# A hybrid decoder layer on one core: one load for the final norm, norm steps spaced wider, output matrices in the buffers of u, and another order of the instructions

## The chip, the cores and the metric

The kernel runs on one core of one Trainium2 chip. Its time is the device time in microseconds of one execution; lower is better. TensorE (PE) multiplies, with its weight loads (PEld) beside it; VectorE (DVE), ScalarE (ACT) and GpSimd (POOL) work elementwise; SyncE (SP) issues most of the transfers (DMA). Each engine takes its instructions in the order of its own list, so an instruction that waits holds up all that stands behind it on that engine.

## The reference

One layer on 16 learned tokens and 2048 given ones, 1024 features, in fp32:

```python
hn = rms_norm(h, norm_mix_g)
b_gate, c_gate, v, u = split(hn @ w_in)             # 512 features each
conv_out = b_gate * causal_dwconv(c_gate * v)        # width 3
ssm_out = s5_group_ssm(u, ...)                       # 32 groups of 16, complex diagonal state of 64, GELU, half-GLU
mixed = concat(rms_norm(conv_out), rms_norm(ssm_out))
h = h + mixed @ w_out
up = causal_dwconv(rms_norm(h, norm_ffn_g) @ w_up) + bias    # 2 x 2816
h = h + (silu(up[:, :2816]) * up[:, 2816:]) @ w_down
y = rms_norm(h, norm_final_g)[:, 16:]
```

## The kernel before

Features lie on partitions, tokens along the free axis. Each fp32 product is three matmuls of rounded halves: with a value split into a high part h_ and the rest l_ (weights: wh_ and wl_), it is h by wh, h's rest by wh, and h by wl's rest (L138, L139, L142 in `product`; L1391 to L1393 in `form`). SP loads raw weights wr_, ACT rounds them to wh_ (L247), DVE subtracts to get wl_ (L109 is the helper `tt` of all DVE's two-operand sums and products). Raw weights have three buffers, split ones four.

The program has these stages. (1) u of block 0, the gated convolution of block 0 (cv, cc, cb, with cvt, vs, tc on DVE) and, beside it, the coefficients of the state space model: tables, transposes tp (L615) copied to tq and written to mat_d in DRAM, then eight slots of products w1, w2 and their difference vm, written to mat_d as well. (2) u and convolution of the other two blocks, with the scan in eight batches 0 to 7 beside it: `ssm_load_out` brings the output matrices mo of a batch, py (L806, L807) multiplies by them. (3) The output projection's convolution part pk, the GLU pg, and the projection po of three token blocks. (4) The gated MLP over three token blocks, each in 22 units of 128 features in groups of 4, 4, 4, 3, 3, 4. `up` of a unit is seven products (b11, t4, t1, t2, b22, b21, t3, a Strassen-like scheme) of 12 matmuls into the PSUM tiles xy and pz; z, g and v are the copies, the convolution and the gate on DVE and ACT, ah and al the split result. After the first unit of the next group, `down` multiplies the finished group (dn); ACT copies it to ev, and POOL adds ev to h_d in DRAM. So a stretch of three or four ups takes turns with one of down.

Norms are generators, run a step at a time between other work (`prep.step`): squares sq summed on DVE, a matmul st with ones, sv, a square root on ACT and POOL (sr), a diagonal dg, a matmul sb that spreads it, rs. A norm's name tells which: c4 is piece of block 2's input, ms and mc the two groups of the mix, f10 the MLP norm of block 1, first half, y00 the final norm of block 0, first half. `prep_rs` makes the sums of the MLP norm, `prep_mlp` scales the four quarters v_b11 to v_b22 of the next block and splits them and their sums (h_t, l_t, h_b, l_b), `finish` makes the final norm of blocks 0 and 1 (`finish_last` that of block 2).

The order of each engine's list does not come from the order of the code alone: a list scheduler places instructions by a model of the engines, with the order of the code as priority.

Of the kernel before, what the change touches and what calls it, by code (L numbers as in the profile page):

```python
# [17 lines left out]
P = 128  # L18
# [39 lines left out]
def layer_kernel(ctx, tc, xq, pk, w_in, w_glu, w_out, w_up, w_down, ssm_s, ssm_m, y):  # L58
# [49 lines left out]
    def tt(out, a, b, op):  # L108
        V.tensor_tensor(out, a, b, op=op)  # L109
# [83 lines left out]
    def inv_rms_at(ss, starts, nfeat, n, name, out=None, keep=False):  # L193
# [8 lines left out]
        for j, o in enumerate(starts):  # L202
            V.tensor_scalar(dg[:sl, o : o + sl], ident[:sl, :sl], r[:sl, j : j + 1], None, op0=ALU.mult)
        yield
        pb = aux_tile(f"sb_{name}")
        T.matmul(pb[:, :n], ones[:sl, :], dg[:sl, :n], start=True, stop=True)
# [7 lines left out]
    def inv_rms_from(srcs, n, name, out=None):  # L214
# [6 lines left out]
        yield  # L221
        if xg is not None:
            yield
            yield
        for t in ts:
# [65 lines left out]

    prep, ssm = Side(), Side()
    SQ = 2

# [429 lines left out]
    def ssm_load_out(b):  # L724
        g0 = b * GB
        mo = a1.tile([P, GB, 2, P], F32, tag="mo", name=f"mo_{b}")
        dma(out=mo, in_=mat_d[:, g0 : g0 + GB, 1:3, :])
        mos[b] = mo

# [68 lines left out]
    def ssm_out(b):  # L798
# [3 lines left out]
        for q in range(PB):  # L802
            ps = mm_tile(f"py_{b}_{q}")
            for par in range(2):
                g = 2 * q + par
                T.matmul(ps[:, par, :NC], mo[:, g, 1, :], ub[:, g, :], start=True, stop=False)  # L806
                T.matmul(ps[:, par, :NC], mo[:, g, 0, :], yy[b][:, q, par, :], start=False, stop=True)  # L807
            S.activation(gb[:, 2 * q : 2 * q + 2, :], ps[:, :, :NC], AF.Gelu_apprx_tanh)
# [267 lines left out]
    prep.add(prep_glu(0, hg[0]), prep_glu(1, hg[1], **xh2))  # L1076
    prep.lanes = 1
    kept = conv_part(0)
# [260 lines left out]
    def finish(b):  # L1339
        for c in range(2):  # L1340
            s0, n = y_at(b, c)
            srcs = [h_d[:, i * 4 : i * 4 + 4, s0 : s0 + n] for i in range(2)]
            rs = yield from inv_rms_from(srcs, n, f"y{b}{c}")
            yield
            for i in range(2):
                a = half_tile(n, f"y_{b}_{c}_{i}", tag="sq", bufs=4)
                dma(out=a, in_=srcs[i])
                yield
                yield
                for k in range(4):  # L1350
# [27 lines left out]
    for b in range(3):  # L1378
# [119 lines left out]
        for ci, (f0, nk) in enumerate(chunk_of):  # L1498
# [3 lines left out]
            for f in range(f0, f0 + nk):  # L1502
                up(f, f == f0 + nk - 1 and ci == last)
                if f == f0 and ci:
                    for ms in first_pair:
                        down(ci - 1, ms)
                        work()
                        prep.step(2 * len(ms))
            if ci == last:
# [122 lines left out]
```

## Time and profile before

| | us |
|---|---|
| median of three runs | 2228.49 (2227.72 to 2231.98) |
| profiled execution | 2233.74 |
| its span | 2232.0 |
| PE busy | 2128.2 |
| DVE busy | 1684.8 |
| ACT busy | 1101.2 |
| mean granted clock of PE | 0.979 |

Busy time of PE counts each matmul from its start to a modelled end, and neighbours overlap, so idle time and waits tell more than the busy share. The profiled execution is 5.2 us above the median, and sums are made against it. In the page's rows a group is a line, engine, operation and tile, with the idle time just ahead of it and what ended that.

### The profile page before, as it was taken

The page shows a single profiled execution, that of the slowest core. Times are in us where ns is not written, and L with a number is a line of the kernel's source. Part 1 is how long each engine was busy: PE and PEld are TensorE (multiplying, and loading weights), DVE is VectorE, ACT ScalarE, POOL GpSimd, SP SyncE. Part 2 cuts the span into 40 slices and gives each one's busy share as a digit, 9 for nine tenths or more (in the row PEclk, how much of TensorE's full clock was granted, in tenths as well). Part 3 has the DMA queues.
Part 4 walks back from the last instruction along what each step waited for, and adds up shares of the span by engine and source line. Part 5 has one row for each costly group of instructions (what it writes and reads, how often), then busy time and mean ns, then how long its engine had stood idle before and what let it go on. Part 6 is the DMA issues. An engine that isn't in the chain of part 4 may idle for free.

```text
span 2232.0 us, 33123 instructions
## 1 busy us (share of the span) xinstructions
PE 2128.2 (95%) x13012; PEld 2065.3 (93%) x13012; DVE 1684.8 (75%) x2507; ACT 1101.2 (49%) x1651; POOL 151.9 (7%) x174
## 2 busy tenths in 40 slices
PE   8997999989899999999999898999998999999997
PEld 7997999989898999999998898999998999999996
DVE  8796499848957798686768777787767879667776
ACT  4135333227523464554555555455555555555554
POOL 0000000000000001101110010100110010110000
PEclk9898999999999999999999999999999999999998
DMA  7376544352475435525554453734554463554463
GB/s 246 99 220 162 135 149 153 113 168 61 141 248 188 149 89 146 130 63 125 127 133 121 120 161 113 211 85 110 129 130 122 125 191 91 134 118 99 100 174 103
DMA packets 174909, 305.85 MB, mean 137 GB/s; under 512 B 32480, under 2 KB 108960, under 8 KB 174624
## 3 DMA queue, kind: packets, MB, share of 16 engines
q1 hardware_dynamic: 154016, 251.98, 36.5%
q0 software_dynamic: 19584, 47.52, 12.7%
q10 hardware_dynamic: 1152, 4.23, 0.5%
q8 instruction: 102, 1.67, 0.3%
q14 instruction: 55, 0.45, 0.1%
HBM read 219.86 MB, written 83.82 MB: 136 GB/s over the span
## 4 chain that ended last, share of the span: by engine, by line
PE 44%; issue 32%; DVE 11%; DMA 6%; POOL 3%; ACT 3%; SPq 0%; POOLq 0%; DVEq 0%; ACTq 0%
PE xy L1391 5%; PE xy L1393 4%; PE xy L1392 4%; PE dn L138 3%; PE dn L139 3%; PE dn L142 3%; POOL h_d L1492 3%; PE pz L1391 2%; PE pz L1393 2%; PE pz L1392 2%; PE po L138 1%; PE po L142 1%; PE po L139 1%; DMA wr_up<-in_w_up 1%; PE cc L138 1%
## 5 line engine op out<-in xcount | busy, mean ns | idle before, releaser
L109 DVE TENSOR_TENSOR wl_up<-wr_up,wh_up 128x1024 fp32r<-128x1024 f32 x198 | 241.5, 1221 | 156.0 <-ACT wh_up L247 154.0
L138 PE MATMUL dn<-ah,wh_dn 128*128 128x344 f32 (+1 forms) x1024 | 326.7, 323 | 10.4 <-ACT ah L247 8.9
L139 PE MATMUL dn<-al,wh_dn 128*128 128x344 f32 (+1 forms) x1024 | 326.0, 322 | 0.1
L247 ACT ACTIVATE wh_up<-wr_up 128x1024 fp32r<-128x1024 f32 x198 | 209.4, 1058 | 207.5 <-PE dn L139 53.9
L1391 PE MATMUL xy<-h_t,wh_up 128*128 128x344 f32 (+1 forms) x792 | 264.5, 334 | 13.3 <-ACT z L1429 7.5
L1393 PE MATMUL xy<-h_t,wl_up 128*128 128x344 f32 (+1 forms) x792 | 254.5, 321 | 0.0
L1392 PE MATMUL xy<-l_t,wh_up 128*128 128x344 f32 (+1 forms) x792 | 254.0, 321 | 0.0
L142 PE MATMUL dn<-ah,wl_dn 128*128 128x344 f32 (+1 forms) x1024 | 247.8, 321 | 0.0
L138 PEld LDWEIGHTS dn<-ah,wh_dn 128*128 128x128 f32 x1024 | 193.9, 190 | 14.8 <-ACT ah L247 9.7
L1492 POOL DMA_DIRECT2D h_d<-ev x136 | 118.3, 870 | 1271.4 <-ACT ev L1488 1266.4
L139 PEld LDWEIGHTS dn<-al,wh_dn 128*128 128x128 f32 x1024 | 194.3, 190 | 1.3 <-DVE al L109 0.8
L1391 PE MATMUL xy<-h_b,wh_up 128*128 128x344 f32 (+1 forms) x528 | 176.5, 336 | 10.6 <-ACT ev L1488 7.9
L1391 PEld LDWEIGHTS xy<-h_t,wh_up 128*128 128x128 f32 x792 | 150.2, 190 | 32.2 <-ACT z L1436 14.9
L142 PEld LDWEIGHTS dn<-ah,wl_dn 128*128 128x128 f32 x1024 | 178.5, 190 | 0.0
L1392 PE MATMUL xy<-l_b,wh_up 128*128 128x344 f32 (+1 forms) x528 | 169.5, 321 | 0.0
L1393 PE MATMUL xy<-h_b,wl_up 128*128 128x344 f32 (+1 forms) x528 | 168.3, 321 | 0.0
L1392 PEld LDWEIGHTS xy<-l_t,wh_up 128*128 128x128 f32 x792 | 150.8, 190 | 0.0
L1393 PEld LDWEIGHTS xy<-h_t,wl_up 128*128 128x128 f32 x792 | 150.7, 190 | 0.0
L247 ACT ACTIVATE wh_dn<-wr_dn 128x512 fp32r<-128x512 f32 (+1 forms) x144 | 85.5, 594 | 124.8 <-issue 43.1
L115 DVE SCALAR_TENSOR_TENSOR g<-z,pv,g 128x688 f32<-128x688 f32 (+1 forms) x132 | 122.0, 925 | 19.6 <-ACT g L1396 18.9
L109 DVE TENSOR_TENSOR wl_dn<-wr_dn,wh_dn 128x512 fp32r<-128x512 f32 (+1 forms) x144 | 92.3, 643 | 48.9 <-ACT wh_dn L247 47.8
L115 DVE SCALAR_TENSOR_TENSOR v<-z,pneg,v 128x688 f32<-128x688 f32 (+1 forms) x132 | 122.2, 926 | 9.3 <-ACT v L1396 8.1
(401 smaller groups left out, 5359.8 us busy)
## 6 DMA issues: line engine op xcount, KB each, us to landing
wr_up<-in_w_up SPq DMA_DIRECT2D x132, 512.0 KB, 5.4
h_d<-ev POOLq DMA_DIRECT2D x88, 344.0 KB, 7.1
wr_dn<-in_w_down SPq DMA_DIRECT2D x96, 256.0 KB, 2.6
wr_cw<-in_w_in SPq DMA_DIRECT2D x36, 512.0 KB, 4.4
h_d<-ev POOLq DMA_DIRECT2D x48, 336.0 KB, 6.6
x_c<-in_xq SPq DMA_DIRECT2D x16, 688.0 KB, 6.0
wr_dn<-in_w_down SPq DMA_DIRECT2D x48, 192.0 KB, 2.4
xr<-in_xq SPq DMA_DIRECT2D x24, 344.0 KB, 4.2
```

What stands on the lines that cost most here:

```text
L109: V.tensor_tensor(out, a, b, op=op)
L115: V.scalar_tensor_tensor(out=out, in0=a, scalar=s, in1=b, op0=ALU.mult, op1=ALU.add)
L138: T.matmul(ps[c], hi[:, k, :], xh, start=k == 0, stop=False)
L139: T.matmul(ps[c], hi[:, k, :], xl, start=False, stop=False)
L142: T.matmul(ps[c], lo[:, k, :], xh, start=False, stop=k == nk - 1)
L247: S.activation(hi, t, AF.Copy)
L1391: T.matmul(ps, hi[:, j, :], xh[:, j, :], start=start and j == 0, stop=False, **kw)
L1392: T.matmul(ps, hi[:, j, :], xl[:, j, :], start=False, stop=False, **kw)
L1393: T.matmul(ps, lo[:, j, :], xh[:, j, :], start=False, stop=j == 3, **kw)
L1492: G.dma_start(out=h_d[:, m, s0 : s0 + no], in_=ev, accum_op=ALU.add)
```

## The change

Five edits in the code, and one in how it is ordered. From `conv_part` on a norm yields once more between dg and sb (`slack`). After its load of h a norm that reads from DRAM always yields four times before it squares. The output matrices mo of odd batches come in two halves into two buffers of u (`ut`), those of even ones into the buffer of mo as before. The final norm of blocks 0 and 1 loads each half of h once, squares it into other tiles (ysq) and scales what it has loaded; before, h was loaded once for the squares and once more to be scaled. Beside down one step of the side work is made for each tile and not two. The last line lets the scheduler place the instructions by a timeline simulation, which changes the order on every engine.

```diff
--- before.py
+++ after.py
@@ -202,6 +202,8 @@
         for j, o in enumerate(starts):
             V.tensor_scalar(dg[:sl, o : o + sl], ident[:sl, :sl], r[:sl, j : j + 1], None, op0=ALU.mult)
         yield
+        if slack:
+            yield
         pb = aux_tile(f"sb_{name}")
         T.matmul(pb[:, :n], ones[:sl, :], dg[:sl, :n], start=True, stop=True)
         if keep:
@@ -219,9 +221,8 @@
             dma(out=ts[i], in_=src)
         yield
         yield
-        if xg is not None:
-            yield
-            yield
+        yield
+        yield
         for t in ts:
             S.activation(t, t, AF.Square)
         a, b = ts
@@ -290,6 +291,7 @@
                 self.step()
 
     prep, ssm = Side(), Side()
+    slack = False
     SQ = 2
 
     class Stream:
@@ -723,9 +725,17 @@
 
     def ssm_load_out(b):
         g0 = b * GB
-        mo = a1.tile([P, GB, 2, P], F32, tag="mo", name=f"mo_{b}")
-        dma(out=mo, in_=mat_d[:, g0 : g0 + GB, 1:3, :])
-        mos[b] = mo
+        if b % 2 == 0:
+            mo = a1.tile([P, GB, 2, P], F32, tag="mo", name=f"mo_{b}")
+            dma(out=mo, in_=mat_d[:, g0 : g0 + GB, 1:3, :])
+            mos[b] = [mo[:, g] for g in range(GB)]
+            return
+        mos[b] = []
+        for i in range(0, GB, 2):
+            t = cvp.tile([P, NJ, 86], F32, tag="ut", bufs=2, name=f"mo_{b}_{i}").rearrange("p j x -> p (j x)")
+            mo = t[:, : 4 * P].rearrange("p (g m c) -> p g m c", g=2, m=2)
+            dma(out=mo, in_=mat_d[:, g0 + i : g0 + i + 2, 1:3, :])
+            mos[b] += [mo[:, 0], mo[:, 1]]
 
     def ssm_in(b):
 
@@ -803,8 +813,8 @@
             ps = mm_tile(f"py_{b}_{q}")
             for par in range(2):
                 g = 2 * q + par
-                T.matmul(ps[:, par, :NC], mo[:, g, 1, :], ub[:, g, :], start=True, stop=False)
-                T.matmul(ps[:, par, :NC], mo[:, g, 0, :], yy[b][:, q, par, :], start=False, stop=True)
+                T.matmul(ps[:, par, :NC], mo[g][:, 1, :], ub[:, g, :], start=True, stop=False)
+                T.matmul(ps[:, par, :NC], mo[g][:, 0, :], yy[b][:, q, par, :], start=False, stop=True)
             S.activation(gb[:, 2 * q : 2 * q + 2, :], ps[:, :, :NC], AF.Gelu_apprx_tanh)
         S.dma_start(out=by_group(g_d)[:, g0 : g0 + GB, :], in_=gb)
 
@@ -1074,7 +1084,7 @@
     hos = [[] for _ in range(3)]
     load_glu()
     prep.add(prep_glu(0, hg[0]), prep_glu(1, hg[1], **xh2))
-    prep.lanes = 1
+    prep.lanes, slack = 1, True
     kept = conv_part(0)
     prep.lanes = 2
     until(hg[0])
@@ -1339,14 +1349,22 @@
     def finish(b):
         for c in range(2):
             s0, n = y_at(b, c)
-            srcs = [h_d[:, i * 4 : i * 4 + 4, s0 : s0 + n] for i in range(2)]
-            rs = yield from inv_rms_from(srcs, n, f"y{b}{c}")
-            yield
-            for i in range(2):
-                a = half_tile(n, f"y_{b}_{c}_{i}", tag="sq", bufs=4)
-                dma(out=a, in_=srcs[i])
+            xs, sq = ([half_tile(n, f"{k}_{b}_{c}_{i}", tag="sq", bufs=4) for i in range(2)] for k in ("y", "ysq"))
+            for i, a in enumerate(xs):
+                dma(out=a, in_=h_d[:, i * 4 : i * 4 + 4, s0 : s0 + n])
+            for _ in range(4):
                 yield
-                yield
+            for a, q in zip(xs, sq):
+                S.activation(q, a, AF.Square)
+            yield
+            q = sq[0]
+            tt(q, q, sq[1], ALU.add)
+            tt(q[:, 0:2, :], q[:, 0:2, :], q[:, 2:4, :], ALU.add)
+            tt(q[:, 0, :], q[:, 0, :], q[:, 1, :], ALU.add)
+            yield
+            rs = yield from inv_rms_of(q[:, 0, :], D, n, f"y{b}{c}")
+            yield
+            for i, a in enumerate(xs):
                 for k in range(4):
                     V.scalar_tensor_tensor(
                         out=a[:, k], in0=a[:, k], scalar=col(C_FIN + 4 * i + k), in1=rs, op0=ALU.mult, op1=ALU.mult
@@ -1505,7 +1523,7 @@
                     for ms in first_pair:
                         down(ci - 1, ms)
                         work()
-                        prep.step(2 * len(ms))
+                        prep.step(len(ms))
             if ci == last:
                 settle()
         if b < 2:
@@ -1624,7 +1642,7 @@
         arrays[f"in_{name}"] = a
         args.append(nc.dram_tensor(f"in_{name}", a.shape, mybir.dt.from_np(a.dtype), kind="ExternalInput").ap())
     out = nc.dram_tensor("out_y", (P, KD, L - META), F32, kind="ExternalOutput").ap()
-    with tile.TileContext(nc) as tc:
+    with tile.TileContext(nc, schedule_with_timeline_sim=True) as tc:
         layer_kernel(tc, *args, out)
     r = _run(nc, [arrays], core_ids=[0])
     yt = np.asarray(r.results[0]["out_y"])
```

Three places of DVE's list. The first is conv block 0, at the split l_c4_0 of the norm of c4 that the matmuls of u of block 2 need (tc and cvt belong to the convolution). Before:

```order
L109 TENSOR_TENSOR vs_0_3_1646<-vs_0_3_1646,rs0_103 128x688
L109 TENSOR_TENSOR wl_u21_1741<-wr_u21_1519,wh_u21_1740 128x1024
L109 TENSOR_TENSOR cvt_0_3_1719<-cc_0_3_1664,vs_0_3_1646 128x688
L903 COPY halo_98<-cvt_0_3_1719 128x2
L115 SCALAR_TENSOR_TENSOR tc_0_3_1724<-cvt_0_3_1719,pv_84,tc_0_3_1724 128x688 x2
L109 TENSOR_TENSOR wr_0_2576<-tab_coarse_1320,tab_fine_1293 128x544
L109 TENSOR_TENSOR tc_0_3_1724<-tc_0_3_1724,rs0_103 128x688
L109 TENSOR_TENSOR l_c4_0_1511<-t_c4_0_1505,h_c4_0_1510 128x4x344
```

And now:

```order
L109 TENSOR_TENSOR vm_924<-w1_919,w2_920 128x32x16
L109 TENSOR_TENSOR w1_919<-bc_150,av_921 128x512
L109 TENSOR_TENSOR w2_920<-bc_150,av_921 128x512
L109 TENSOR_TENSOR vm_924<-w1_919,w2_920 128x32x16
L109 TENSOR_TENSOR w1_919<-bc_150,av_921 128x512
L109 TENSOR_TENSOR w2_920<-bc_150,av_921 128x512
L109 TENSOR_TENSOR vm_924<-w1_919,w2_920 128x32x16
L109 TENSOR_TENSOR wr_0_2576<-tab_coarse_1320,tab_fine_1293 128x544
L109 TENSOR_TENSOR wi_0_2577<-tab_coarse_1320,tab_fine_1293 128x544
L801 MEMSET sb_0_2755 128x4
L109 TENSOR_TENSOR l_c4_0_1511<-t_c4_0_1505,h_c4_0_1510 128x4x344
```

The last five of the eight vm slots now stand between the convolution's rows and l_c4_0; before, all eight stood ahead of the convolution's last piece. The split moved behind them, and behind wi_0.

The second is the last up of MLP block 0, unit 21, whose al is what the last group of down waits for; l_t2, l_b22, l_b21 and l_t4 are splits for block 1. Before:

```order
L115 SCALAR_TENSOR_TENSOR v_0_21_11168<-z_0_21_1_11040,pneg_6806,v_0_21_11168 128x672
L109 TENSOR_TENSOR l_t1_1_11301<-v_b11_1_10579,h_t1_1_11300 128x4x344
L115 SCALAR_TENSOR_TENSOR v_0_21_11168<-z_0_21_1_11040,pneg_6806,v_0_21_11168 128x672
L1159 SCALAR_TENSOR_TENSOR v_b11_1_10579<-v_b11_1_10579,v_b22_1_10581 128x4x344
L109 TENSOR_TENSOR v_0_21_11168<-g_0_21_11169,v_0_21_11168 128x672
L109 TENSOR_TENSOR l_t3_1_11461<-v_b12_1_10580,h_t3_1_11460 128x4x344
L109 TENSOR_TENSOR al_0_21_11188<-v_0_21_11168,ah_0_21_11187 128x672
L109 TENSOR_TENSOR l_t2_1_11306<-v_b11_1_10579,h_t2_1_11305 128x4x344
L109 TENSOR_TENSOR l_b22_1_11386<-v_b22_1_10581,h_b22_1_11385 128x4x344
```

And now:

```order
L109 TENSOR_TENSOR l_b22_1_11394<-v_b22_1_10589,h_b22_1_11393 128x4x344
L109 TENSOR_TENSOR l_t3_1_11469<-v_b12_1_10588,h_t3_1_11468 128x4x344
L109 TENSOR_TENSOR l_b21_1_11432<-v_b21_1_10590,h_b21_1_11431 128x4x344
L115 SCALAR_TENSOR_TENSOR v_0_21_11176<-z_0_21_1_11048,pneg_6814,v_0_21_11176 128x672
L109 TENSOR_TENSOR l_t4_1_11353<-v_b11_1_10587,h_t4_1_11352 128x4x344
L115 SCALAR_TENSOR_TENSOR v_0_21_11176<-z_0_21_1_11048,pneg_6814,v_0_21_11176 128x672
L109 TENSOR_TENSOR v_0_21_11176<-g_0_21_11177,v_0_21_11176 128x672
L109 TENSOR_TENSOR al_0_21_11196<-v_0_21_11176,ah_0_21_11195 128x672
```

The splits of block 1 that followed al_0_21 now stand ahead of it; the same holds at the end of block 1.

The third is up 2 of MLP block 1. Before:

```order
L115 SCALAR_TENSOR_TENSOR g_1_0_11664<-z_1_0_0_11498,pv_84,g_1_0_11664 128x688
L109 TENSOR_TENSOR sq_y00_0_11619<-sq_y00_0_11619 128x336
L109 TENSOR_TENSOR z_1_0_1_11499<-xy_1_0_11500,z_1_0_1_11499 128x688
L109 TENSOR_TENSOR wl_up1_1_3_11614<-wr_up1_1_1_11418,wh_up1_1_3_11613 128x1024
L115 SCALAR_TENSOR_TENSOR g_1_0_11664<-z_1_0_0_11498,pv_84,g_1_0_11664 128x688
L109 TENSOR_TENSOR wl_up1_2_0_11655<-wr_up1_2_0_11493,wh_up1_2_0_11654 128x1024
L109 TENSOR_TENSOR wr_up1_2_0_11493<-wr_up1_2_0_11493,wr_up1_2_1_11568 128x512
L115 SCALAR_TENSOR_TENSOR v_1_0_11663<-z_1_0_1_11499,pneg_6806,v_1_0_11663 128x688
L109 TENSOR_TENSOR wr_up1_2_1_11568<-wr_up1_2_1_11568,wr_up1_2_0_11493 128x512
L115 SCALAR_TENSOR_TENSOR v_1_0_11663<-z_1_0_1_11499,pneg_6806,v_1_0_11663 128x688
```

And now:

```order
L203 TENSOR_SCALAR dg_y00_12316<-ident_75,sr_y00_12274 112x112
L109 TENSOR_TENSOR z_1_0_0_11506<-xy_1_0_11508,z_1_0_0_11506 128x344
L203 TENSOR_SCALAR dg_y00_12316<-ident_75,sr_y00_12274 112x112 x2
L109 TENSOR_TENSOR wl_up1_1_3_11622<-wr_up1_1_1_11426,wh_up1_1_3_11621 128x1024
L115 SCALAR_TENSOR_TENSOR g_1_0_11674<-z_1_0_0_11506,pv_84,g_1_0_11674 128x688 x2
L109 TENSOR_TENSOR z_1_0_1_11507<-xy_1_0_11508,z_1_0_1_11507 128x688
L109 TENSOR_TENSOR wl_up1_2_0_11665<-wr_up1_2_0_11501,wh_up1_2_0_11664 128x1024
L1369 SCALAR_TENSOR_TENSOR y_0_0_0_11627<-y_0_0_0_11627,pv_84,rs_y00_12398 128x336 x4
L1369 SCALAR_TENSOR_TENSOR y_0_0_1_11628<-y_0_0_1_11628,pv_84,rs_y00_12398 128x336 x4
L109 TENSOR_TENSOR wr_up1_2_0_11501<-wr_up1_2_0_11501,wr_up1_2_1_11576 128x512
L115 SCALAR_TENSOR_TENSOR v_1_0_11673<-z_1_0_1_11507,pneg_6814,v_1_0_11673 128x688
```

The final norm of block 0 (dg_y00 and the scaling y rows) now stands among the weights and gates of the first ups; before, only its squares did, and the rest stood beside the down group that follows.

## The prediction

> **What bounds the kernel now.** I read the page's head first, then who waited for whom on PE, then busy time in chosen stretches, then DVE's groups by shape.
>
> ```profile
> span 2232.0 us, 33123 instructions
> PE 2128.2 (95%) x13012; PEld 2065.3 (93%) x13012; DVE 1684.8 (75%) x2507; ACT 1101.2 (49%) x1651; POOL 151.9 (7%) x174
> ```
>
> TensorE (PE) is busy for 95% of the span, so only its idle 104 us, and any clock lost with it, can be won; all else can only be lost. The waits view says whom PE waited for (total us, times, longest):
>
> ```profile
> PE dn L138 <- ACT ah L247: 8.9, 3, 3.4
> PE xy L1391 <- ACT ev L1488: 7.9, 2, 4.1
> PE xy L1391 <- ACT z L1429: 7.5, 2, 7.1
> PE py L806 <- DMA mo<-mat_d: 6.8, 1, 6.8
> PE sb_mc L206 <- DVE dg_mc L203: 4.6, 3, 3.8
> PE st_c L188 <- DVE sq_c L109: 4.5, 2, 3.3
> PE pu L138 <- ACT h_c L247: 4.4, 2, 4.0
> PE po L138 <- DVE xr L109: 3.7, 1, 3.7
> PE sb_c L206 <- DVE dg_c L203: 3.6, 2, 2.9
> PE st_f L188 <- DVE sq_f L109: 3.6, 1, 3.6
> PE xy L1391 <- ACT z L1436: 2.6, 1, 2.6
> PE st_ms L188 <- DVE sq_ms L109: 1.8, 1, 1.8
> PE pk L142 <- DVE wl_o L109: 1.7, 1, 1.7
> ```
>
> Nearly all are norm work (st, sb, dg, sq) or single late transfers. The stretches (length, then PE, PEld, DVE, ACT, POOL busy with counts, granted clock, DMA share, GB/s) show where there is room:
>
> ```profile
> 159.00:178.00 19.00, 7.90 (x40) 6.08 (x38) 15.96 (x28) 6.78 (x8) 1.20 (x1) 0.74 0.68 215
> 539.00:603.00 64.00, 57.05 (x335) 53.94 (x336) 56.70 (x88) 34.13 (x37) 6.10 (x6) 0.95 0.34 107
> 751.00:822.00 71.00, 67.57 (x411) 64.89 (x411) 64.25 (x83) 48.49 (x72) 0.00 (x0) 0.98 0.38 123
> 856.00:909.00 53.00, 52.10 (x326) 50.23 (x325) 48.52 (x66) 30.27 (x50) 0.86 (x1) 1.00 0.30 78
> 909.00:941.00 32.00, 31.89 (x207) 31.50 (x206) 16.88 (x22) 14.37 (x22) 6.05 (x7) 1.00 0.73 164
> 1168.00:1199.00 31.00, 31.00 (x198) 30.23 (x197) 30.51 (x38) 19.57 (x33) 0.00 (x0) 1.00 0.22 60
> 1249.00:1299.00 50.00, 47.39 (x285) 46.09 (x284) 43.79 (x57) 32.24 (x59) 0.00 (x0) 0.97 0.22 67
> 1749.00:1796.00 47.00, 47.00 (x292) 45.61 (x291) 44.57 (x59) 31.90 (x52) 0.00 (x0) 1.00 0.25 74
> ```
>
> The row at 856 is four up projections, the row at 909 one down group. Beside up, VectorE (DVE) is busy 48.5 of 53 us: it is nearly as full as PE. Beside down it is busy 16.9 of 32. So DVE has room beside down and almost none beside up, and what the new order puts on DVE beside up, PE pays for. The row at 909 also gives PE's pace: 32.0 us / 207 = 0.155 us a matmul.
>
> **The change, part by part.** DVE's rows, by shape (count, busy us, mean ns), price what moves:
>
> ```profile
> L109 DVE TENSOR_TENSOR w<-bc,av 128x512 f32<-128x512 f32 x14 | 9.0, 680 | 0.0
> L240 DVE SCALAR_TENSOR_TENSOR t_c<-x_c,pv,rs_c 128x344 f32<-128x344 f32 x16 | 8.0, 570 | 2.1 <-ACT rs_c L211 2.1
> L109 DVE TENSOR_TENSOR l_c<-t_c,h_c 128x1376 fp32r<-128x1376 f32 x4 | 6.2, 1587 | 0.0
> L109 DVE TENSOR_TENSOR wl_u<-wr_u,wh_u 128x1024 fp32r<-128x1024 f32 x4 | 4.9, 1215 | 0.0
> L115 DVE SCALAR_TENSOR_TENSOR tc<-cvt,pv,tc 128x688 f32<-128x688 f32 x4 | 3.7, 928 | 0.8 <-ACT tc L905 0.7
> L109 DVE TENSOR_TENSOR l_t<-v_b,h_t 128x1376 fp32r<-128x1376 f32 x8 | 12.7, 1589 | 2.4 <-ACT h_t L247 2.4
> L1129 DVE SCALAR_TENSOR_TENSOR v_b<-v_b,pv,rsk 128x344 f32<-128x344 f32 x32 | 16.4, 570 | 4.2 <-DMA v_b<-h_d 2.6 <-ACT rsk L211 1.6
> L1351 DVE SCALAR_TENSOR_TENSOR y<-y,pv,rs_y 128x344 f32<-128x344 f32 x16 | 8.4, 570 | 1.4 <-ACT rs_y L211 1.4
> L109 DVE TENSOR_TENSOR sq_f<-sq_f,sq_f 128x1376 f32<-128x1376 f32 x4 | 6.3, 1587 | 0.4 <-ACT sq_f L226 0.4
> L109 DVE TENSOR_TENSOR sq_f<-sq_f 128x688 f32<-128x688 f32 x4 | 3.5, 866 | 0.0
> L203 DVE TENSOR_SCALAR dg_f<-ident,sr_f 115x115 f32<-115x115 f32 x12 | 3.5, 317 | 2.6 <-POOL sr_f L199 2.5
> L109 DVE TENSOR_TENSOR w_up<-wr_up,wr_up 128x512 f32<-128x512 f32 x66 | 45.5, 690 | 1.6
> ```
>
> A row that follows another starts before the one ahead has ended: in the chain of waits four y rows take 1.92 us, 0.08 us less each than their mean. I take 0.08 off every row.
>
> ```profile
> 1318.38 1.92 DVE y L1351 x4
> 1345.12 1.35 ACT L226 ACTIVATE sq_f<-sq_f 128x1376 f32<-128x1376 f32 x1 [10.32 <-DMA sq_f<-h_d]
> mat_d<-vm SPq DMA_DIRECT2D x2, 1024.0 KB, 6.3
> mo<-mat_d SPq DMA_DIRECT2D x8, 512.0 KB, 6.9
> y<-h_d SPq DMA_DIRECT2D x4, 688.0 KB, 10.4
> ```
>
> *Gains.* **mo.** With two halves in the u buffers the loads of odd batches no longer wait for the single buffer; the 6.8 us of py and the 1.7 of wl_o behind it should go, with about 1 us of clock: between -6 and -10, I take -9. **Norms after the scan.** In the new order the st and sb matmuls of ms, mc and the first MLP norm stand 30 to 85 matmuls behind what they need, where 11 to 25 stood: 85 x 0.155 = 13 us of cover. The waits st_ms 1.8, sb_mc 4.6, po 3.7 and st_f 3.6 make 13.7, and the clock of 0.95 over 64 us another 3.2. DVE is 89% busy there, so some lateness stays: -6 to -20, I take -13. **One load of h.** It takes 4 x 0.69 MB of reads from each of two blocks. The longest wait, 7.1 us of xy for z, is the row at 1345: ACT stood 10.32 us at the head of its queue for sq_f, whose load was issued behind the second reading of h. That form goes: -3 to -9, I take -8. **Steady ups.** The copies out of PSUM stand further ahead of the matmuls that wait for them; at 856 PE idles 0.9 us in 53, so 66 ups (13.3 us each) hold 15 us at most: 0 to -15, I take -6, since other splits now stand closer. The waits of xy for ev (7.9) I leave as they are (down to -7.9). Together -36.
>
> *Losses.* **Start.** A square of the first norm stands ahead of the first weight split on ACT: +1.3 by the row at 1345 (0 to +2).
>
> **Conv block 0.** The coefficients' transposes are spread out, so the vm rows come later and stand ahead of l_c4. From the cvt row of the block's last piece to l_c4_0 DVE now has 15 w and vm rows (10.2 us), two wl_u (2.4), eight t_c (4.6), four tc (3.6), cvt, wr and wi (2.3, from the like shapes) and l_c4_0 (1.6): 24.7, less 31 x 0.08, is 22.2 us. PE has 53 matmuls there, 8.2 us: 14 us late. On to l_c5_0, 32 matmuls (5.0 us) face 12.7 us of rows: 7.7 more, 21.7 in all. Before, PE waited 4.5 + 3.6 + 4.4 = 12.5 here, for the same norms. That is +9; and wi now waits until vm's tile has been written out (6.3 us, with 1.4 of cover): +14. I take +12, range +6 to +19. If the cover were gone too, SP's queue, with the weights of u behind it, would come next.
>
> **First ups of the MLP.** The norm of block 1 (16 v_b rows 9.1 us, four sq rows some 3.5, six dg 1.9) and four late rows of block 0 (two l_t, two sums of like size, 6.4) are added from 751 to 822: 20.9, less 30 x 0.08, is 18.5. DVE has 71 - 64.25 = 6.75 free: +11.8. I take +11 (+5 to +14; below if rows not needed at once slip behind those that are).
>
> **Last up of blocks 0 and 1.** Four l rows (6.4) that stood behind al of unit 21 now stand ahead, and four weight sums (2.8) fall into the same stretch: 8.6 us after overlap, where DVE is busy 30.51 of 31.00. dn of the last group waits for that al. Some of it is covered by the wait for ah that is there already (8.9 in three places, two of these): +7 each, +14 (+4 to +18).
>
> **First ups of blocks 1 and 2.** The final norm now runs beside up. Block 1: 16 y rows (9.0), one more set of sq rows (3.0), four sq_f (4.5), nine dg (2.9): 19.4, less 33 x 0.08, is 16.8 against 50 - 43.79 = 6.2 free: +10.6; I take +9 (+3 to +13). Block 2: the same without the norm of a next block, 14.0 less 2.0 is 12.0, against 47 - 44.57 = 2.4: +9.6; I take +8 (+3 to +10). The down groups that lose the work gain nothing: DVE has 15 us free in each.
>
> Losses 1.3 + 12 + 11 + 14 + 9 + 8 = 55.3; net +19.3. The profiled execution took 2233.74 us (span 2232.0 and 1.7 around it): 2253. It lies 5.2 us above the median of the runs, 2228.49, so the median comes to **2248 us**.
>
> **The clock.** In the row at 159, where PE waited in single pieces of 3 to 4 us, the granted clock is 0.74; at 1249, where the longest wait is 2.6 us, it is 0.97, or 1.5 us lost. [...]
>
> **Rivals.** *Faster: splits run far enough ahead.* Up's weights are split into four buffers, so DVE may fall behind by about one up before PE sees it. Then the lateness beside up shrinks from 28 to 5 us and at the last ups from 14 to 6, while the gains come in full with the waits for ev: 1.3 + 12 + 5 + 6 - 36 - 8 = -20: 2209. It decides if wl stands over 10 us (65 matmuls) ahead of its matmul when the norm rows begin. Against it: in the new order wl_up1_2_1 stands right behind the y and ysq rows, and its matmul is the next that PE needs. *No difference:* gains at their upper bounds (9.5 + 20 + 9 + 15) against my losses, 2228 to 2232. *Much slower: transfers at a queue's head.* ACT squares y and sq_f beside up as soon as their turn comes, and loads of y took 10.4 us, sq_f's wait 10.32. If such a wait of 7 us meets three of the stretches, 21 more: 2269. It decides where a load is issued less than its landing time ahead; the 7.1 us wait of before speaks for it, the smaller traffic against. That "thinner beside down" does not happen is no rival but part of the forecast: the rows stand beside up.
>
> **How the numbers follow.** Forecast 0.45, faster 0.27, no difference 0.08, much slower 0.20. Changes under 0.2% (4.5 us) cannot be told from none. Of the forecast's 0.45 a little reaches over to the other side (its terms spread some 15 us): 0.62 slower, 0.08 same, 0.30 faster. The likeliest case alone spans 2233 to 2263; the range for all, cutting a tenth at each end, is 2212 to 2282.
>
> **What would show it.** Right: no wait of py for mo; PE waits for l_c4 or h_c4 near 160 us; DVE over 95% busy in the first ups of each block, PE waiting there for wl_up or z; dn waiting for ah or al 8 us or more at the last ups. Wrong: DVE below 90% there with PE at 98%, or a sum of PE's idle below 104 us. What would overturn it most easily is the size of the losses beside up, since all three hang on DVE having no room.

## The result, and the profile after

The changed kernel takes **2296.76 us** (median of four runs, 2295.72 to 2301.57), the one before 2228.78 on the same chip. The ratio is **1.0306, interval 1.0293 to 1.0318**: 3.1% slower. The forecast, 2248 in a range of 2212 to 2282, has the direction and less than a third of the size: 19 us, where the medians differ by 68. The profiled execution has a span of 2294.2 us, 62.2 more than before, and a mean granted clock of 0.965, where it was 0.979. (The profiled execution of before lies 5 us above its median, that of after 1 us below; so the traces show 62 us and the medians 68.)

The head of the page after:

```profile
span 2294.2 us, 33152 instructions
PE 2134.2 (93%) x13012; PEld 2081.0 (91%) x13012; DVE 1674.0 (73%) x2507; ACT 1099.4 (48%) x1651; POOL 155.9 (7%) x174
```

PE makes as many matmuls as before and is busy 6.0 us longer, at the lower clock. Its idle time grew from 103.8 to 160.0 us, and that is nearly all of the loss. DVE has 10.8 us less to do than before: no work was added, work was moved. Whom PE waited for (total us, times, longest):

```profile
PE dn L138 <- ACT ah L248: 17.4, 5, 7.2
PE pu L138 <- DVE wr L109: 12.8, 1, 12.8
PE pu L139 <- DVE l_c L109: 11.7, 3, 10.0
PE pu L138 <- ACT wh_u L248: 11.6, 1, 11.6
PE xy L1409 <- ACT wh_up L248: 10.8, 13, 2.4
...
PE pz L1409 <- ACT h_t L248: 6.6, 1, 6.6
...
PE po L139 <- DVE l_ms L109: 4.0, 2, 2.0
PE pu L138 <- DVE ut L109: 3.9, 1, 3.9
...
PE st_ms L188 <- DVE sq_ms L109: 2.3, 2, 1.2
...
PE pg L138 <- ACT kp L1064: 1.9, 1, 1.9
PE po L138 <- ACT h_ms L1038: 1.7, 2, 1.3
```

Behind the wait for the first weights, the list of before was led by ah, the copies ev and z, and one late transfer (mo). This one is led by splits: of ah (17.4, where it was 8.9), of c4 (the wr and l_c rows), of up's weights (wh_up 10.8 in 13 pieces). The waits for mo, ev and the 7.1 us wait for z are gone. The stretches in order of time (length, then PE, PEld, DVE, ACT, POOL busy with counts, granted clock, DMA share, GB/s) are the wait for c4, the first ups of MLP block 0, its last up and the wait of dn behind it, and the first ups of blocks 1 and 2:

```profile
176.00:186.00 10.00, 1.23 (x3) 0.79 (x3) 1.02 (x4) 1.46 (x2) 0.00 (x0) 0.50 0.97 258
806.00:868.00 62.00, 57.87 (x346) 55.43 (x346) 59.35 (x91) 35.01 (x60) 2.52 (x2) 0.94 0.25 80
1201.00:1242.00 41.00, 35.86 (x210) 33.48 (x208) 38.73 (x44) 27.38 (x40) 0.00 (x0) 0.96 0.18 53
1242.00:1272.00 30.00, 22.91 (x137) 22.91 (x138) 15.66 (x18) 10.59 (x16) 6.05 (x7) 0.89 0.63 135
1296.00:1350.00 54.00, 45.97 (x264) 43.00 (x262) 51.78 (x78) 31.95 (x53) 3.64 (x2) 0.92 0.49 160
...
1808.00:1860.00 52.00, 44.01 (x264) 41.08 (x263) 50.80 (x75) 30.34 (x49) 1.16 (x1) 1.00 0.29 99
```

In the three rows of first ups (806, 1296, 1808) DVE is busy 96, 96 and 98% and PE only 93, 85 and 85%. Beside down, in the row at 1242, DVE has half its time free. That is the room which the work left. In the row at 806 PE's waits come to 4.0 us in all; the larger ones of that stage lie ahead of it (h_t 6.6, l_t 2.4).

**Where the 62 us arise.** For each of two traces I took the time at which the last matmul of a named tile ends, subtracted those of before, and took the difference from one stage's end to the next's. Each column is one profiled execution, so parts of 1 to 2 us mean little. Negative is a gain, and all columns behind "after" are experiments of the next section: "three holds" is its last kernel (scan, norms and splits held), "two holds, old order" the kernel before with norms and splits held.

| stage (its last tile) | forecast | after | order alone | edits alone | norms held | splits held | three holds | two holds, old order |
|---|---|---|---|---|---|---|---|---|
| start (pu of block 0) | +1.3 | +9.0 | +7.2 | 0.0 | +7.6 | +7.4 | +8.0 | +0.1 |
| to the last convolution (cb of block 2) | +12 | +21.2 | +22.8 | +1.2 | +20.8 | +20.8 | +11.2 | -2.0 |
| py (first pk) | -9 | -11.5 | -3.2 | -7.6 | -11.6 | -11.5 | -11.5 | -0.4 |
| output projection (last po) | -13 | +2.9 | -5.0 | +0.6 | -0.1 | -0.2 | +0.2 | -0.1 |
| first ups, block 0 (xy_0_5) | +11 | +18.0 | +15.2 | -4.1 | +11.1 | +18.5 | +10.9 | +1.5 |
| last up, block 0 (last dn) | +7 | +8.0 | +6.1 | +1.1 | +7.6 | -4.0 | -4.0 | -3.2 |
| first ups, block 1 (xy_1_5) | +9 - 8 | +5.9 | +20.7 | -12.6 | -17.8 | +5.8 | -16.6 | -16.4 |
| last up, block 1 (last dn) | +7 | +7.3 | +7.3 | -0.3 | +6.8 | -5.4 | -5.4 | -3.9 |
| first ups, block 2 (xy_2_5) | +8 | +12.8 | +17.3 | +1.8 | -4.9 | +9.9 | -4.8 | -4.9 |
| steady ups, three blocks | -6 | -10.0 | -7.1 | +9.4 | -3.8 | -13.6 | -9.5 | +3.9 |
| end | 0 | -1.4 | -2.6 | -1.2 | -3.6 | -2.3 | -3.1 | -0.5 |
| sum | +19.3 | +62.2 | +78.7 | -11.7 | +12.1 | +25.4 | -24.6 | -25.9 |

The clock that is lost in a stage is in its figure. With the edits alone, the 12.6 us won in the first ups of block 1 are mostly given back in the steady ups (+9.4).

### The profile page after: what moved, and what is told of

It reads as the page before. It is cut to its first block, busy times and chain, and to the rows that moved or that the text cites. A ratio compares the mean times of both kernels' runs of the same rounds, so it can differ in the third digit from the quotient of the medians.

```text
span 2294.2 us, 33152 instructions
## 1 busy us (share of the span) xinstructions
PE 2134.2 (93%) x13012; PEld 2081.0 (91%) x13012; DVE 1674.0 (73%) x2507; ACT 1099.4 (48%) x1651; POOL 155.9 (7%) x174
## 4 chain that ended last, share of the span: by engine, by line
PE 56%; DVE 13%; ACT 4%; DMA 3%; issue 2%; POOL 0%; SPq 0%; POOLq 0%; DVEq 0%; ACTq 0%
PE dn L138 7%; PE xy L1409 7%; PE xy L1411 7%; PE dn L139 7%; PE dn L142 7%; PE xy L1410 7%; PE pz L1409 3%; PE pz L1410 3%; PE pz L1411 3%; PE po L142 1%; PE po L139 1%; PE po L138 1%; DVE wl_up L109 1%; ACT wh_up L248 1%; DVE g L115 1%
## 5 line engine op out<-in xcount | busy, mean ns | idle before, releaser
L138 PE MATMUL dn<-ah,wh_dn 128*128 128x344 f32 (+1 forms) x1024 | 328.7, 326 | 23.7 <-ACT ah L248 17.4
L1409 PE MATMUL xy<-h_b,wh_up 128*128 128x344 f32 (+1 forms) x528 | 171.7, 325 | 6.5 <-ACT z L1456 3.9
L109 DVE TENSOR_TENSOR z<-xy,z 128x688 f32<-128x688 f32 (+3 forms) x132 | 91.0, 690 | 54.9 <-PE xy L1411 54.1
```

The source lines that it names most:

```text
L138: T.matmul(ps[c], hi[:, k, :], xh, start=k == 0, stop=False)
L1409: T.matmul(ps, hi[:, j, :], xh[:, j, :], start=start and j == 0, stop=False, **kw)
```

## The experiments

My theory after the result: the order makes the loss, because it puts norm rows and splits, which nobody needs yet, on DVE and ACT ahead of rows that PE is about to need. The rivals were that one of the edits makes it, or that the transfers which the edits move do.

**The order alone, and the edits alone.** The one is the kernel before with a single line changed, the other has the five edits and the order as before:

```diff
-    with tile.TileContext(nc) as tc:
+    with tile.TileContext(nc, schedule_with_timeline_sim=True) as tc:
```

> The code of before, with only the other way of ordering. Theory A (the order makes the loss, and the edits of the code give a little back): the row order on DVE at conv block 0, at the last ups and in the first ups is nearly that of the change, so 2295 to 2310 us. Rival B (the edits make the loss, since they let norm work run beside up, and the order alone is worth the 19 us that the prediction summed): 2235 to 2255.

> The five edits of the code, ordered as before. Theory A: the three places of DVE's list read as before, so 2205 to 2225 us: 8 less for mo, some 8 less for the wait of xy behind the second reading of h, nothing for the rest. Rival B: 2250 or more.

The order alone took 2311.55 us against 2231.41, 1.0359 (1.0344 to 1.0375). The edits alone took 2221.1, 0.9957 (0.9943 to 0.9972). So the order costs more than the whole change does, and the edits gain about as much under it as without it. PE's longest items with the order alone are those of the changed kernel:

```profile
PE xy L1391 <- ACT wh_up L247: 22.6, 14, 5.8
PE dn L138 <- ACT ah L247: 17.2, 3, 7.0
PE pu L138 <- DVE wr L109: 12.8, 1, 12.8
```

With the edits alone, four of the first ups of block 1 have no wait left:

```profile
1249.00:1299.00 50.00, 50.00 (x311) 48.75 (x311) 45.89 (x61) 31.40 (x57) 0.00 (x0) 1.00 0.22 69
```

The long wait for z has moved, though, and not gone. Before, PE waited 7.1 us at 1348 behind ACT's 10.32 us for the load of sq_f; now ACT stands 7.58 us for another load of sq_f, 78 us later, and PE waits 6.9 us behind it, at 1424:

```profile
PE xy L1409 <- ACT z L1447: 7.4, 2, 6.9
1422.63 1.35 ACT L227 ACTIVATE sq_f<-sq_f 128x1376 f32<-128x1376 f32 x1 [7.58 <-DMA sq_f<-h_d]
```

**Two edits, each alone** in the kernel before: `finish` with its one load of h, and the matrices mo in the buffers of u.

```diff
-                dma(out=a, in_=srcs[i])
+                dma(out=a, in_=h_d[:, i * 4 : i * 4 + 4, s0 : s0 + n])
...
+            for a, q in zip(xs, sq):
+                S.activation(q, a, AF.Square)
```

```diff
+        if b % 2 == 0:
...
+            t = cvp.tile([P, NJ, 86], F32, tag="ut", bufs=2, name=f"mo_{b}_{i}").rearrange("p j x -> p (j x)")
```

> Before with the final norm's one load alone. Prediction's term: the wait of 7.1 us in block 1 goes, 2218 to 2224 us. Rival: the squares wait for other loads instead, 2228 within 3.

> Before with the output matrices of odd batches in the u buffers alone. Prediction's term: py no longer waits 6.8 us, 2219 to 2222 us. Rival: the gain shows at py and is lost again at the next late row (gt, wl_o), 2226 to 2229.

One load took 2230.18 us against 2231.41, 0.9998 (0.9988 to 1.0008); mo took 2229.17, 0.9994 (0.9983 to 1.0004). Neither does anything that can be measured, and in both it was the rival that came, though each wins what it was to win where it works: by the traces one load is 6.2 us ahead in the first ups of block 1, mo 7.5 us at the first pk. By the same traces each gives most of it back at a later place that was not ready to start earlier. These are single executions, and that of mo took 2237.35 us, 8 above its median, so which place takes the gain is less sure than that it goes. With one load that is the first ups of block 2 (+5.8), where PE waited longest for this:

```profile
PE st_y L188 <- DVE ysq L109: 3.2, 1, 3.2
```

With mo it is pg and the norms beside it (+4.4 to the last po):

```profile
PE sb_mc L206 <- DVE dg_mc L203: 3.8, 1, 3.8
PE pg L142 <- DVE wl_g L109: 2.3, 1, 2.3
```

**Parts of the new order undone.** The order cannot be mixed by hand, so I moved or held single groups of instructions in the changed kernel. `issue_after` puts an instruction behind a named one in the list of the same engine; it adds no wait. The named ones of the norms and splits are on ACT (`mark[0]` is the copy ev, `act["ins"]` the rounding of ah), so ACT's squares and roundings are held, and DVE's rows come later because they read those. A priority of 400 lets the scheduler treat an instruction as if it stood 400 earlier in the code. First, the coefficients' steps early:

```diff
+                    with tc.high_priority(offset=self.ahead):
+                        end = next(g, self) is self
...
+    ssm.ahead = 400
     ssm.add(coefficients())
```

Second, the norms beside down: no step beside up, two for each tile beside down, and each behind the copy ev of the group at hand. These are three changes in one, and the two steps undo the fifth edit; they were not tried one by one.

```diff
-            if f < f0_last:
-                prep.step()
...
-                        S.activation(two(ev), whole[m], AF.Copy)
+                        mark[0] = S.activation(two(ev), whole[m], AF.Copy)
...
-                        prep.step(len(ms))
+                        prep.after = mark[0]
+                        prep.step(2 * len(ms))
+                        prep.after = None
```

Third, the next block's splits behind ah of unit 21 (its al then comes ahead of them on DVE too):

```diff
             hf[b + 1]["go"] = True
+            prep.after = act["ins"]
             for ms in [(0, 1, 2)] + [(m,) for m in range(3, KD)]:
                 down(last, ms)
                 prep.step(len(ms))
             prep.drain()
+            prep.after = None
```

> The change, with the coefficients' steps (transposes and vm slots) given a higher priority, so that all eight vm slots stand ahead of the convolution's last piece on DVE again. Theory A (the late vm slots, with the wait of wi for their transfer behind them, make the loss near 180 us): the stage is 20 to 28 us shorter, 2270 to 2278 us. Rival: DVE is full there in any order, and the lateness moves ahead into the convolution: 2288 or more.

> The change, with the squares of the final norms and of the MLP norms of blocks 1 and 2 held until a down group has been copied out, so that no norm row stands in the first ups. Theory A (DVE has no room beside up): the first ups of the three blocks win 8 to 15 us each, 2262 to 2275 us. Rival (the weights' splits are late beside up in this order whatever stands between them): 2290 to 2300.

> The change, with the splits of the next block held until ah of unit 21 has been made. Theory A: the waits for ah and al at the last ups fall from some 12 us to 3 each, 2278 to 2283 us. Rival: the held splits are then late in the first up of the next block, and no more than 5 us remain: 2291 to 2297.

> The change with all three holds. If the three losses lie in places of their own, the gains add up: 24 + 28 + 16 less than the change, 2225 to 2240 us. Rival: one lateness is carried into the next place, so that the sum falls short by 20 or more: 2250 to 2270.

Against 2232.35 us of the kernel before, the three took 2277.24 (1.0199, 1.0184 to 1.0215), 2246.71 (1.0061, 1.0046 to 1.0076) and 2258.34 (1.0113, 1.0098 to 1.0128). All three together took **2208.17, 0.9888 (0.9871 to 0.9904)**: faster than the kernel before, and better than both of the expected ranges. Each hold gives back much of what its stages had lost, and two give more than I expected. With the norms held, the first ups of block 1 go from +5.9 to -17.8 and those of block 2 from +12.8 to -4.9; their rows and all that PE waited for from 1263 to 1385 us are

```profile
1282.00:1330.00 48.00, 47.47 (x298) 46.72 (x297) 45.85 (x60) 30.26 (x56) 0.00 (x0) 1.00 0.21 67
1763.00:1812.00 49.00, 47.98 (x300) 46.96 (x300) 44.74 (x57) 30.02 (x50) 0.00 (x0) 1.00 0.22 67
```

```profile
PE xy L1413 <- ACT wh_up L248: 0.5, 2, 0.3
PE xy L1413 <- ACT z L1460: 0.4, 1, 0.4
```

PE is 98 to 99% busy where it was 85. DVE is still 91 to 96% busy in these rows: what changed is which rows it works on, and what ACT stands for. With the splits held the last ups gain 4.0 and 5.4 us on the kernel before, where the changed kernel lost 8.0 and 7.3. From 1195 to 1275 us 0.8 us of the wait for ah is left, and over the whole run

```profile
PE dn L138 <- ACT ah L248: 4.8, 3, 3.4
```

The kernel before had waits at these places too (ah, and the 7.1 us for z), and the holds shorten them as well; but there another cause is at work, which I had left out. ACT takes its list in order, and it stood for loads of h into the squares of the norms:

```profile
ACT sq_y L226 <- DMA sq_y<-h_d: 11.9, 4, 6.3
ACT sq_f L226 <- DMA sq_f<-h_d: 10.5, 2, 10.3
```

This is the kernel before from 1200 to 1500 us, with DVE busy only 43.79 of 50 us in the first ups of block 1. PE's waits of 4.1 (ev), 2.6 and 7.1 us (z) there end just after ACT's stands of 6.3, 2.6 and 10.3. With the two holds under the old order no square of the MLP waits more than 1.5 us for its load. So a hold does two things, it frees DVE and lets the loads land first, and the runs do not separate them: in the old order the second is what the traces show, in the new one both are there (ACT stood 9.2 us in two pieces for y and 5.5 in four for sq_f).

**What the edits add to the holds.** The kernel before with the two holds of the MLP (norms and splits) and no edit; the same with the edits (but for the fifth, which the norm hold undoes); and all three holds under the new order, but with two loads of h.

> The code of before with the two holds alone, no edit and the order as before. If DVE's place beside down is what counts, nearly all of the win is here: 2195 to 2208 us. Rival (what wins is the one load of h, held): within 4 of 2228.

> The five edits and the two holds in the MLP (norms until a down group has been copied out, the next block's splits until ah of unit 21 is made), with the order made as before, where the start and conv block 0 lose nothing. If the holds win in the MLP what they win in the changed order, block by block (some 30 us from the first up of block 0 on, against before), this ends at 2185 to 2200 us. Rival (the win of the holds needs the copies out of PSUM to stand as far ahead as the changed order puts them): 2210 to 2222, as the five edits alone.

> The change with all three holds, but the final norm loads h twice as before. Beside down the y loads took 10 us to land; if the second reading still costs a wait where the norm stands beside down, 5 to 9 us more than with one load (2213 to 2217). Rival: hidden, within 3 of 2208.

Against 2230.52 us: the holds alone took 2209.95, 0.9911 (0.9894 to 0.9927), just above the expected 2195 to 2208. With the edits it was 2208.52, 0.9904 (0.9887 to 0.9921), where I had expected 2185 to 2200. With two loads it was 2209.31, 0.9908 (0.9891 to 0.9924), no different from 2208.17 with one; the rival came. The gains do not add: in the first ups of block 1 the edits alone win 12.6 us, the holds alone 16.4 and both 17.9, out of the same idle time. Why the edits' 4 us in the first ups of block 0 (-4.1, and -0.1 with the holds) is lost as well I did not find.

**What made the wait in conv block 0.** DVE's timeline there (start, length, count at the end, idle before it in brackets):

```profile
173.49 1.29 DVE L109 TENSOR_TENSOR w<-bc,av 128x512 f32<-128x512 f32 x2
174.82 0.69 DVE L109 TENSOR_TENSOR vm<-w,w 128x512 f32<-128x512 f32 x1
175.55 0.73 DVE L109 TENSOR_TENSOR wr<-tab_coarse,tab_fine 128x544 f32<-128x544 f32 x1
185.25 0.73 DVE L109 TENSOR_TENSOR wi<-tab_coarse,tab_fine 128x544 f32<-128x544 f32 x1 [8.98 <-DMA mat_d<-vm]
185.91 1.58 DVE L109 TENSOR_TENSOR l_c<-t_c,h_c 128x1376 fp32r<-128x1376 f32 x1
```

ACT's timeline there, and the view of tile vm with its transfers:

```profile
174.87 2.59 ACT L248 ACTIVATE h_c<-t_c 128x1376 fp32r<-128x1376 f32 x2 [8.01 <-DVE w L109]
```

```profile
L661 SPq DMA_DIRECT2D mat_d<-vm x2: 359/1054/1749, 175.5 to 175.9; - x2
...
DMA to landing us min/median/max: 5.2/7.2/9.2
```

Two waits stop PE in turn. t_c of c4 is ready at 164 us, but its high part h_c is rounded only at 174.87, when the last w row has ended, since h_c of c4 lies in a pool that is opened when the pool of the coefficients (bc, av, w, vm) is closed. That is PE's wait of 12.8 us; the view puts it down to wr, which ended 0.01 us before. Then l_c stands behind wi, and wi waits 8.98 us for vm's two transfers, issued at 175.5 and 175.9 and landed after 5.2 and up to 9.2: PE's second wait, of 10.0. Before, ACT rounded the same tile at 153.06, with all vm rows long done. With the coefficients early the rounding follows the t_c rows with no idle time:

```profile
164.18 2.59 ACT L248 ACTIVATE h_c<-t_c 128x1376 fp32r<-128x1376 f32 x2
```

There this part of the program gains 17 us, but the start pays 6.6 more for it. To separate the transfer from the pool, the next kernel holds only the scan's first rows (wr, wi and what follows from them) behind the last split of the input of block 1 (l_c of c3); the vm rows stay as they are:

```diff
     u_block(2, hu, last=True)
     until(hc[1], 2)
+    ssm.after = last_lo[0]
```

> The change, with the scan's first rows (wr, wi, ct, st of batch 0) held behind the splits of the norm of c3, so that wi no longer stands ahead of l_c4 with its wait for vm's transfer; the vm slots stay where the change has them. Theory A1 (the transfer's 9 us are a part of their own beside the late slots): 9 us and the clock lost with them less, 2283 to 2288 us. Rival (the slots alone make l_c4 late, the next norms would have waited anyway): 2293 or more.

> The change with the hold of the scan's first rows and the two holds of the MLP, without the priority for the coefficients (which cost 6.6 us at the start). If the parts are separate: the nine-tenths of a per cent that the three holds before had below the kernel before, less the 6.6 us at the start, and up to 5 more where the slots stay late: 2203 to 2213 us. Rival: more than 2218.

It took 2285.97 us against 2229.96, 1.0259 (1.0232 to 1.0285): by the two ratios about 10.5 us less than the changed kernel, and of PE's two waits the second is gone:

```profile
PE pu L138 <- ACT h_c L250: 20.8, 3, 12.8
PE pu L139 <- DVE l_c L109: 2.1, 3, 0.8
```

So the wait for the transfer is a part of its own, worth 10 us. The other 12.8 now stand under h_c's name, as they should, but they are not the pool's alone. In this run DVE goes from its last vm row to l_c with hardly a stop:

```profile
173.04 0.69 DVE L109 TENSOR_TENSOR vm<-w,w 128x512 f32<-128x512 f32 x1
174.47 3.09 DVE L109 TENSOR_TENSOR l_c<-t_c,h_c 128x1376 fp32r<-128x1376 f32 x2 [0.74 <-ACT h_c L250]
```

Had h_c been free at once, l_c could have come 0.74 us earlier at most, since the late vm rows stand ahead of it on DVE in any case. The pool decides under which name the wait is seen; the late vm rows make it, by their place on DVE and by the pool that they keep. This hold with the two of the MLP took 2207.86, **0.9901 (0.9885 to 0.9916)**, in the 2203 to 2213 that I expected. Five kernels thus come to 0.989 to 0.991 with intervals that overlap, and the kernel before needs only the two holds for it.

## Why the prediction was right and wrong

**Right in kind.** The losses beside up are where the forecast put them: DVE at 96 to 98%, PE waiting for wh_up, z and wl_up, dn for ah. The step "what the new order puts on DVE beside up, PE pays for" holds for the norms as a whole, since the norm hold shows that the same rows beside down cost little or nothing; that DVE alone is the reason is not shown, as the hold moves ACT's squares and their loads too. The two last ups were +8.0 and +7.3 against "+7 each". Of what was to show the steps right, four things came: no wait of py for mo, PE's wait for c4 near 160 us, DVE over 95%, dn waiting 8.0 us for ah at the end of block 0 and 9.2 for ah and al at the end of block 1.

**Start, +9.0 against +1.3.** The term counted one square on ACT. That part was right in size (PE's first wait, for wh_u, went from 9.8 to 11.6 us). Left out was DVE: PE waited 3.9 us for ut, the raw u that DVE writes out, behind rows of the coefficients. The order alone has +7.2, so it is the order. The two waits make 5.7; behind the second the granted clock falls to 0.50, with PE busy and only 20 matmuls in 6 us, which is about the rest of the 9.0 (before, it stayed at 1.00 here):

```profile
45.00:51.00 6.00, 5.70 (x20) 5.73 (x21) 3.95 (x28) 0.00 (x0) 0.00 (x0) 0.50 0.93 153
```

**Conv block 0, +21 to the last convolution against +12.** The row count was nearly right, and two other steps failed. The first is the credit: "Before, PE waited 4.5 + 3.6 + 4.4 = 12.5 here, for the same norms" was taken off, but those waits did not go. From 150 to 260 us PE now waits 37.4 us, of which 22.8 are for c4 (12.75 and 10.05) and 14.6 for the norms behind it; before, all its waits there made 14.7. So the 22.8 came on top. The forecast had 14 + 4.9 for c4, and for the rest 7.7 less 12.5. The second is the transfer: "6.3 us, with 1.4 of cover" was the median of two, 5.2 and 7.5, that were issued 4.2 us apart. Now they are issued 0.4 us apart, the second lands after 9.2, and wi waited 8.98 us, 4 more than was summed. The place was no quieter before (a DMA share of 1.01 from 141 to 153 us). The pool was in no sum either, but by the run with the scan's first rows held it moves l_c by less than a microsecond.

**mo, -11.5 against -9,** but worth nothing in the end. Alone it gave 0.9994; under the new order the output projection takes back what py gained (order alone -3.2 then -5.0, with the edits -11.5 then +2.9). "Should go" was right for the wait and wrong for the time.

**Norms after the scan, +2.9 against -13:** the largest single error, 16 us. "85 x 0.155 = 13 us of cover" is true of the st and sb matmuls, and their waits did shrink (sb_mc's 4.6 is gone from the list, po's 3.7 for xr too). But I priced the cover of a norm's sums and not what the same rows then hold up: po waited 4.0 us for l_ms and 1.7 for h_ms, pg 1.9 for kp, st_ms still 2.3. The lateness moved one step on, from the norm's sums to its splits.

**First ups.** Block 0 cost +18.0 against +11, and mostly for another reason: pz waited 6.6 us for h_t and 2.4 for l_t, the splits of block 0's own first operand, and the clock was at half from 779 to 792 us. What the norm hold gives back here, 6.9 us, is all that is shown of the norm rows. Blocks 1 and 2 cost +5.9 and +12.8 against +1 and +8. The "free" time in DVE's row was taken as usable to the last, and ACT, which rounds wh_up and stood for the loads of y and sq_f, was in no sum.

**One load, -8.** In its place it is worth 6.2 us (alone), or 14.8 together with the other edits (order alone +20.7, all +5.9), and over the whole kernel nothing that can be measured: 0.9998 alone, and 2208.17 against 2209.31 beside the holds. The step "That form goes" was wrong: with the edits alone ACT still stands 7.58 us for sq_f, at a later place.

**Steady ups, -10.0 against -6:** within its bounds of 0 to -15.

**Rivals.** *Faster* asked that the splits run over 10 us ahead of their matmuls. They did not: PE waited 13 times for wh_up at xy alone. *Much slower, transfers at a queue's head* had the right mechanism and too large a price beside up. ACT did stand for the loads of y and sq_f, 4.8 us at the longest where 7 were supposed, and the three rows of first ups have no wait of PE of over 3 us; with the order alone, which still loads h twice, ACT stood 22.8 us in five pieces for sq_y. The late transfer that hurt most was vm's, in conv block 0. *No difference* would have needed the edits' gains in full, and they are worth 0.4%.

**The clock.** The two waits of dn at the end of blocks 0 and 1 came; the row at 1242, with one of 7.2 us, has a clock of 0.89, which is some 3 us lost in 30. None of the forecast's losses has a term for it. The last section shows a place where short waits, 1.55 us at most, went with a fall of the clock as well.

**Open.** How the gain of the holds divides between room on DVE and loads that ACT no longer stands for is not shown. The three holds under the new order (scan, norms, splits) lose about 8 us up to the last po (8.0 + 11.2 - 11.5 + 0.2) and gain 32.5 after it; the two holds under the old order gain 2.4 and 23.5. A kernel with the start of the one and the MLP of the other would be some 9 us faster still by this sum of two single executions. It was not tried, as the order is made for the whole program at once.

## What to carry to other kernels

Before you move work, find the stretches in which the engines that prepare operands have no time left, or would stand for a transfer, and keep all that is not needed at once out of them: two groups of instructions held back until then gained 1% here, while the five edits to transfers, buffers and steps gained 0.4%. A wait that is removed is worth only what the next place can take: follow each to where the gain is given back before counting it, and take nothing off a forecast for a wait that the change does not touch. And when an order is made by a model, look beyond the lists at transfers and memory: wi stood 9 us for a tile that was still being written out, which no row count shows, and ACT stood 8 us ahead of h_c, whose tile lies in a reused pool, until the last row that read what lay there had ended.

## What the runs showed of the hardware that was not expected

**The clock fell without any wait of over 1.55 us.** PE's timeline of the changed kernel in the first ups of block 1, only two rows with idle time ahead of them and one of the first at the slower pace:

```profile
1309.90 0.42 PE L1409 MATMUL xy<-h_t,wh_up 128*128 128x344 f32 x1 [1.05 <-ACT wh_up L248]
...
1312.04 0.43 PE L1409 MATMUL pz<-h_b,wh_up 128*128 128x344 f32 x1 [1.55 <-ACT wh_up L248]
...
1314.40 0.49 PE L1409 MATMUL xy<-h_t,wh_up 128*128 128x344 f32 x1
```

The busy time around it, and at a like place in block 2 (the rows from 1310.95 and 1850.30 are explained below):

```profile
1309.00:1314.00 5.00, 2.07 (x8) 1.21 (x8) 5.00 (x7) 5.00 (x8) 0.00 (x0) 1.00 0.15 28
1310.95:1314.37 3.42, 1.73 (x7) 1.15 (x8) 3.42 (x4) 3.42 (x6) 0.00 (x0) 1.00 0.32 75
1314.00:1318.00 4.00, 3.87 (x15) 3.87 (x16) 4.00 (x6) 2.34 (x4) 0.00 (x0) 0.57 0.87 293
...
1850.30:1853.72 3.42, 1.72 (x11) 1.44 (x10) 3.42 (x6) 1.21 (x4) 0.00 (x0) 1.00 0.89 320
1852.00:1860.00 8.00, 4.52 (x23) 3.68 (x24) 8.00 (x12) 6.43 (x11) 0.00 (x0) 1.00 0.28 94
```

No wait was over 1.55 us, yet after 5 us with PE 41% busy a matmul took 0.49 us (at 1314.40) in place of 0.32 (at 1313.41) and the granted clock was 0.57 over the next four. From 1852 to 1860 PE was 57% busy, also in short pieces (no wait over 1.70 us), and the clock stayed at 1.00 (as it did in the twelve us after). So here it was the share of idle time in a few us, not one long gap, that went with the loss. The traces tell more, since they record every change of the granted clock. In those of before and after it is either 1.00 or 0.50, and every change lies at a multiple of 3.41 us from the first one recorded (to within 0.005 us). Cut at these points, the two traces have 25 stretches of 3.41 us at full clock in which PE was busy less than 45%, and all 25 were followed by one at half clock; of 1198 in which it was busy 60% or more, two were, both where PE makes the small products kps; in between, 11 of 19. The stretches from 1310.95 and from 1850.30 are of that middle: PE is busy 51 and 50% in them, the first cost the clock and the second did not. So here short waits cost the clock in places where they left PE idle for about half of such a stretch, and not in each; what decided between these two is not shown. (PE's busy time is partly modelled, so the bounds are no sharper than this.)

**Two transfers of the same size, issued 0.4 us apart, landed after 5.2 and 9.2 us** (vm's, 1 MB each, at a DMA share of 0.97 and 258 GB/s in the row at 176). Before, the same two were issued 4.2 us apart at as high a share (1.01, and 255 GB/s, from 141 to 153 us), and landed after 5.2 and 7.5:

```profile
L659 SPq DMA_DIRECT2D mat_d<-vm x2: 359/825/1291, 141.3 to 145.5; - x2
...
DMA to landing us min/median/max: 5.2/6.3/7.5
```

At 258 GB/s 1 MB takes some 4 us (an estimate from that row), about what lies between the two landings (0.4 + 9.2 - 5.2 = 4.4), as if the second had waited for the first; that it did is not shown. The median of 6.3 was 3 us short for wi, which waits for both.
